# First stage of a hybrid SSD and gated-MLP layer: even rows' weights in two pieces around h, a pair's ada chunks in one burst, the pair's last chunk in two transfers, fewer warm-up matmuls

## The chip, the core and the metric

The kernel runs on one core of a Trainium2 chip. The metric is the device time of one execution in microseconds (us); the median of three runs of the kernel before is 986.98 us. The core has five engines that run side by side: TensorE (PE: matmuls; PEld is its weight load), VectorE (DVE), ScalarE (ACT), GpSimd (POOL) and SyncE (SP), which here only issues DMA transfers. All transfers run on 16 DMA engines that the queues share.

## The reference, cut to what matters

One layer works on 256 latent tokens `x` and 256 context tokens `ctx`, with 2048 features each.

```
shift, scale, gate       = split(silu(c)     @ w_ada + b_ada, 3)
shift_c, scale_c, gate_c = split(silu(c_ctx) @ w_ada + b_ada, 3)
hc = rmsnorm(ctx, g_pre) * (1 + scale_c) + shift_c
zc = hc @ w_in[:, :XBC_W + DT_W]
hx = rmsnorm(x, g_pre) * (1 + scale) + shift
zx = hx @ w_in
# then a convolution, two SSD scans, a gated MLP and the output projection
```

Everything is in float32. The kernel gets its precision by splitting each factor of a product into a rounded high part and a low part (`hi`, `lo`), and sums three products of the parts.

## The kernel before, in words

**The first stage** holds about the first 125 us. It makes the modulation (`shift` and `scale` for 16 slices of 128 features), the normalized input `h` of both token groups (512 columns), and the first seven output tiles of `w_in` with the 64 `dt` columns. It runs over 16 rows (`kt`): row k is the contraction over the features of slice k, and all its tiles add up in PSUM (`psdt` for the `dt` columns, `psx0` to `psx5` for the seven tiles, numbered 0 to 6 below; tiles 3 and 6 have 256 columns and share the bank `psx3`, the others 512). Behind it come the other tiles of `w_in`, the scans and the output projection; the change does not touch them.

**Data.** Four transfers bring the tokens (`xT`), 32 transfers of 1 MiB the columns of `w_ada` for shift and scale (`ada_0` to `ada_31`, "chunks"), 16 of 480 KB the rows' weights (`wst0` to `wst15`). SP issues them in the order of the program. Chunks lie in six buffers, rows' weights in three, and a transfer waits for its buffer.

**Modulation.** Rows 0 to 3 have two chunks each (`ada_rows`, step `r`, then `k`, `g`, `o`). From row 4 on, a pair of rows (4 and 5, 6 and 7, ...) has four. The first goes through VectorE as eight products with an accumulated sum (`ada_part`, step `v`, line 262) and a bias (`b`, line 268). The other three go through TensorE (`ada_mm`, step `a`, line 253, tile `psada`). `ada_fin` (step `f`, lines 275 and 278) transposes the result and adds the two shares into `hab`, the scale and shift of both rows of the pair.

**One row.** `scale_x` (`x`, line 388) multiplies `xT` by the norm. `make_h` (`h`, line 395: four halves on ACT) or `make_hs` (`hs`, lines 401 and 402: two halves on ACT, two on VectorE) writes `hhi` and the full value into `xT`. `make_hl` (`e`, line 405) writes `hlo`, their difference. `split_hi` (`c`, line 377) casts the row's weights, `split_dt` (`d`, line 381) and `split_lo` (`l`, line 385) write low parts. TensorE then runs `psdt` (line 455), the first three tiles (`p` and `q`, lines 475 to 478) and the tiles 3 to 6 (`m`, lines 143 to 145).

**What sets the order.** Inside the stage the engines' orders are the program's own (`manual_schedule`). `row_steps(kt)` lists the steps that are written out during row kt: the row's own matmuls and the preparation of row n = kt + 1. `m0` is `psdt` and the first three tiles, `m1` tiles 3 to 6. For an odd kt, row n is the first of a pair.

**Before the rows**, TensorE sums the squares of `xT` (line 341) and runs warm-up matmuls between them (`warm`, tile `psw`, line 319).

Of the kernel before, what the change touches and what calls it, by code (L numbers as in the profile page):

```python
# [11 lines left out]
AF = mybir.ActivationFunctionType  # L12
ALU = mybir.AluOpType
# [4 lines left out]
KT = D // P  # L18
# [29 lines left out]
def tile_hybrid_ssd_mlp(  # L48
# [30 lines left out]
    def load_raw(src, name):  # L79
        raw = wp["raw"].tile([P, 2048], F32, tag="raw", name=name)  # L80
        nc.sync.dma_start(raw, src)
        return raw
# [47 lines left out]
    hab = stp.tile([P, KT, 2, 2], F32, name="hab")  # L130
# [7 lines left out]
    hhi = [hpool.tile([P, TOK], F32R, name=f"hhi{k}") for k in range(KT)]  # L138
# [17 lines left out]
    def yseg(j):  # L156
        return y[:, j // 4, (j % 4) * 512 : (j % 4 + 1) * 512]
# [6 lines left out]
    zt, e = yseg(5)[:, 0:256], yseg(5)[:, 256:512]  # L164
# [12 lines left out]
    xT = stx.tile([P, KT, TOK], F32, name="xT")  # L177
# [15 lines left out]
    ada_raw = {}  # L193
# [62 lines left out]
    def ada_part(u, i):  # L256

        q, v = divmod(i, 2)
        if i == 0:
            part[u] = ada_raw.pop(4 * u - 2 * NSING), st2.tile([P, 4, 2], F32, tag="part", name=f"part{u}")  # L260
        raw, acc = part[u]
        nc.vector.scalar_tensor_tensor(cbj, raw[:, q * 512 : (q + 1) * 512], 1.0, cb[v], op0=ALU.mult, op1=ALU.mult,
                                       accum_out=acc[:, q, v : v + 1])
# [23 lines left out]
    def wst_load(kt):  # L287
        w = st3.tile([P, WST], F32, tag="wst", name=f"wst{kt}")
        nc.sync.dma_start(w, wst[kt])
        wraw[kt] = w  # L290

    for t in range(4):
        nc.sync.dma_start(xT[:, 4 * t : 4 * t + 4, :].rearrange("p k t -> p (k t)"), xch[t])

    ada_load(0)

    def ada_load2(c):
        ada_raw[c] = raw = wp["raw"].tile([P, 2048], F32, tag="raw", name=f"ada_{c}")
        for hf in range(2):
            nc.sync.dma_start(raw[:, hf * 1024 : (hf + 1) * 1024], wada[c][:, hf * 1024 : (hf + 1) * 1024])  # L300
# [16 lines left out]
    def warm(*ns):  # L317
        for n in ns:
            nc.tensor.matmul(psw[:, 0:n], lhsT=ones, rhs=ones[:, 0:1].to_broadcast([P, n]), start=True, stop=True)  # L319
# [53 lines left out]
    def split_hi(kt, a=0, b=WST):  # L373
        if a == 0:
            sp0[kt] = (wp["spl"].tile([P, WST + 64], F32R, tag="hi", name=f"hi_st{kt}"),
                       wp["spl"].tile([P, WST - 64], F32R, tag="lo", name=f"lo_st{kt}"))
        nc.scalar.copy(sp0[kt][0][:, 64 + a : 64 + b], wraw[kt][:, a:b])  # L377
# [5 lines left out]
    def split_lo(kt, a=64, b=WST):  # L383
        hi, lo = sp0[kt]
        nc.vector.tensor_tensor(lo[:, a - 64 : b - 64], wraw[kt][:, a:b], hi[:, 64 + a : 64 + b].bitcast(F32), op=ALU.subtract)
# [2 lines left out]
        nc.vector.scalar_tensor_tensor(xT[:, kt, :], xT[:, kt, :], pc[:, C_GPRE + kt : C_GPRE + kt + 1], rb,  # L388
                                       op0=ALU.mult, op1=ALU.mult)

    def make_h(kt):
        sl = (slice(256, 512), slice(0, 256))
        for t in (hhi[kt], xT[:, kt, :]):
            for v, s in enumerate(sl):
                nc.scalar.activation(t[:, s], xT[:, kt, s], AF.Identity, bias=hab[:, kt, 1, v : v + 1],
                                     scale=hab[:, kt, 0, v : v + 1])

    def make_hs(kt):
        a, b = hab[:, kt, 0], hab[:, kt, 1]
        for t in (hhi[kt], xT[:, kt, :]):  # L400
            nc.scalar.activation(t[:, 256:512], xT[:, kt, 256:512], AF.Identity, bias=b[:, 0:1], scale=a[:, 0:1])
# [92 lines left out]
    scale_x(2)  # L494
    for kt in range(KT):
        cs = (2 * kt + 6, 2 * kt + 7) if kt + 3 < KT else ()
        if kt < NSING - 2:
            wst_load(kt + 2)
        ada_load(*cs)
        if NSING - 2 <= kt < KT - 2:  # L500
            wst_load(kt + 2)
        for what, i in row_steps(kt):
            step(kt, what, i)
        if kt == 6:
            nc.scalar.dma_start(dtc, dtp[0:1].partition_broadcast(P))
            nc.scalar.dma_start(A, dtp[1:2].partition_broadcast(P))
            nc.scalar.dma_start(dsk, dskip.partition_broadcast(P))
# [625 lines left out]
    for blk in range(16):  # L1133
# [46 lines left out]
    op1 = ctx.enter_context(mkpool(name="op1", bufs=1))  # L1180
# [36 lines left out]
    for i in range(8):  # L1217
        tk, b = divmod(i, 4)
# [156 lines left out]
```

## Time and profile before

| What | Value |
|---|---|
| Three runs | 986.9, 986.98, 988.93 us |
| The profiled execution, its own time | 987.21 us |
| Its span | 985.5 us |
| TensorE busy | 977.1 us (99%) |
| VectorE, ACT busy | 655.8 us, 501.9 us |
| First psdt of row 0, of row 15 | 22.91 us, 122.61 us |
| DMA in 40 to 60 us | 418 GB/s, share 1.01 |

The span is that of the instructions; 1.7 us of the execution's time lie around it. Matmuls are pipelined, so a row's duration (0.39 us for 512 columns) is longer than the step from one start to the next (0.23 us), and PE counts as busy while it waits a little. Starts are therefore what to compare. In a row of the time line stand the start in us, the duration in us (for "x2" of both), engine, line, operation, what is written and read, shapes, and in brackets idle time of the engine with what ended it.

### The profile page before, as it was taken

To read this page: it belongs to the slowest core of one execution; us is meant where nothing else is said; L and a number is where in the kernel's file an instruction comes from. 1 tells how busy PE (TensorE), PEld (TensorE's weight loads), DVE (VectorE), ACT (ScalarE), POOL (GpSimd) and SP (SyncE) were. 2 spreads that over 40 slices of the span, in tenths; PEclk is the share of its full clock that TensorE was granted. 3 is DMA by queue.
4 is the path that set the end of the run, shared out by engine and by line. 5 is a ranking of instruction groups with operands and counts; after the bars stand their busy time and mean duration, and the time that the engine had idled before them with its cause. 6 is when DMAs were issued, how large, how long until landed. Compare 5 with 4: busy or idle time off the path is not lost.

```text
span 985.5 us, 13637 instructions
## 1 busy us (share of the span) xinstructions
PE 977.1 (99%) x5310; PEld 786.6 (80%) x5310; DVE 655.8 (67%) x1041; ACT 501.9 (51%) x758; POOL 112.5 (11%) x162
## 2 busy tenths in 40 slices
PE   9999999999999999999999999999999999999997
PEld 3778888778887878787888888887888888888885
DVE  5887798768886665756767766767555564445636
ACT  4344458566565454645444434555565563345522
POOL 0000002532462122124000000000000000000000
PEclk9999999999999999999999999999999999999999
DMA  9999943232323423146788777764455545556722
GB/s 372 419 418 415 388 153 134 97 144 103 128 90 134 161 85 129 44 171 217 296 304 281 283 269 270 296 259 171 170 190 195 175 167 213 188 197 231 281 86 86
DMA packets 31985, 207.26 MB, mean 210 GB/s; under 512 B 4128, under 2 KB 4384, under 8 KB 8496
## 3 DMA queue, kind: packets, MB, share of 16 engines
q1 hardware_dynamic: 28800, 192.71, 52.1%
q0 software_dynamic: 2112, 12.65, 3.7%
q10 hardware_dynamic: 1008, 1.02, 0.3%
q8 instruction: 42, 0.69, 0.3%
q14 instruction: 23, 0.19, 0.1%
HBM read 204.20 MB, written 2.16 MB: 209 GB/s over the span
## 4 chain that ended last, share of the span: by engine, by line
PE 96%; DVE 1%; ACT 1%; issue 0%; ACTq 0%
PE pa L1152 12%; PE pa L1154 12%; PE pa L1153 12%; PE psx L143 9%; PE psx L145 9%; PE psx L144 9%; PE pm L1199 3%; PE pm L1201 3%; PE pm L1200 3%; PE pq L1201 2%; PE pq L1200 2%; PE pq L1199 2%; PE psada L253 2%; PE psc L822 1%; PE pso L875 1%; PE psw L319 1%
## 5 line engine op out<-in xcount | busy, mean ns | idle before, releaser
L88 DVE TENSOR_TENSOR lo_w<-w,hi_w 128x1024 fp32r<-128x1024 f32 x173 | 210.3, 1223 | 142.1 <-ACT hi_w L87 142.0
L87 ACT CAST hi_w<-w 128x1024 fp32r<-128x1024 f32 x173 | 182.1, 1053 | 204.0 <-PE pa L1154 132.7
L1152 PE MATMUL pa<-hi_w,hhi 128*128 128x512 f32 x512 | 202.3, 395 | 0.0
L1154 PE MATMUL pa<-hi_w,hlo 128*128 128x512 f32 x512 | 199.5, 390 | 0.0
L1153 PE MATMUL pa<-lo_w,hhi 128*128 128x512 f32 x512 | 199.3, 389 | 0.0
L143 PE MATMUL psx<-hhi,hi_w 128*128 128x512 f32 (+1 forms) x400 | 153.4, 383 | 0.0
L145 PE MATMUL psx<-hhi,lo_w 128*128 128x512 f32 (+1 forms) x400 | 145.9, 365 | 0.0
L144 PE MATMUL psx<-hlo,hi_w 128*128 128x512 f32 (+1 forms) x400 | 145.7, 364 | 0.0
L1152 PEld LDWEIGHTS pa<-hi_w,hhi 128*128 128x128 f32 x512 | 96.2, 188 | 20.5 <-issue 1.6
L1154 PEld LDWEIGHTS pa<-hi_w,hlo 128*128 128x128 f32 x512 | 96.1, 188 | 20.3
L1153 PEld LDWEIGHTS pa<-lo_w,hhi 128*128 128x128 f32 x512 | 96.2, 188 | 19.4 <-issue 0.2
L620 DVE SCALAR_TENSOR_TENSOR xbc<-psx,pc,xbc 128x248 f32<-128x248 f32 (+1 forms) x204 | 83.6, 473 | 34.8 <-ACT xbc L604 33.8
L545 DVE TENSOR_TENSOR lo_w<-w,hi_w 128x1024 fp32r<-128x1024 f32 x61 | 77.1, 1271 | 23.6 <-ACT hi_w L539 23.6
L143 PEld LDWEIGHTS psx<-hhi,hi_w 128*128 128x128 f32 x400 | 75.5, 189 | 13.4 <-issue 2.9
L145 PEld LDWEIGHTS psx<-hhi,lo_w 128*128 128x128 f32 x400 | 75.4, 188 | 12.5
L144 PEld LDWEIGHTS psx<-hlo,hi_w 128*128 128x128 f32 x400 | 75.6, 189 | 12.2 <-issue 1.7
L539 ACT CAST hi_w<-w 128x1024 fp32r<-128x1024 f32 x61 | 63.5, 1044 | 26.0 <-PE psx L144 12.9
L1010 DVE SCALAR_TENSOR_TENSOR junk<-gate,cb 128x2048 bf16<-128x2048 f32 x16 | 36.7, 2292 | 26.3 <-DMA gate<-in_wada_dram 26.3
L1199 PE MATMUL pm<-hi_w,hhi 128*128 128x512 f32 x128 | 50.0, 390 | 0.0
L1200 PE MATMUL pm<-lo_w,hhi 128*128 128x512 f32 x128 | 49.9, 390 | 0.0
L1201 PE MATMUL pm<-hi_w,hlo 128*128 128x512 f32 x128 | 49.6, 389 | 0.0
L377 ACT CAST hi_st<-wst 128x960 fp32r<-128x960 f32 (+2 forms) x17 | 16.0, 942 | 45.0 <-DMA wst<-in_wst_dram 45.0
(269 smaller groups left out, 1395.7 us busy)
## 6 DMA issues: line engine op xcount, KB each, us to landing
w<-in_wlat_dram SPq DMA_DIRECT2D x64, 1024.0 KB, 4.8
w<-in_wout_dram SPq DMA_DIRECT2D x32, 1024.0 KB, 4.8
ada<-in_wada_dram SPq DMA_DIRECT2D x30, 1024.0 KB, 12.6
w<-in_wxbc_dram SPq DMA_DIRECT2D x25, 1024.0 KB, 4.8
gate<-in_wada_dram SPq DMA_DIRECT2D x16, 1024.0 KB, 5.6
R<-acs POOLq DMA_DIRECT2D x8, 1024.0 KB, 5.0
wst<-in_wst_dram SPq DMA_DIRECT2D x15, 480.0 KB, 11.9
xT<-in_xch_dram SPq DMA_DIRECT2D x4, 1024.0 KB, 7.9
```

The costliest lines, as they stand in the source:

```text
L87: nc.scalar.copy(hi, raw)
L88: nc.vector.tensor_tensor(lo, raw, hi.bitcast(F32), op=ALU.subtract)
L143: nc.tensor.matmul(ps, lhsT=whi, rhs=hhi[k][:, s], start=start, stop=False)
L144: nc.tensor.matmul(ps, lhsT=whi, rhs=hlo[k][:, s], start=False, stop=False)
L145: nc.tensor.matmul(ps, lhsT=wlo, rhs=hhi[k][:, s], start=False, stop=stop)
L620: nc.vector.scalar_tensor_tensor(ao, zi, cw[:, k : k + 1], ao, op0=ALU.mult, op1=ALU.add)
L1152: nc.tensor.matmul(pa[tk], lhsT=hhi[k][:, t], rhs=whi[:, w], start=k == 0, stop=False)
L1153: nc.tensor.matmul(pa[tk], lhsT=hhi[k][:, t], rhs=wlo[:, w], start=False, stop=False)
L1154: nc.tensor.matmul(pa[tk], lhsT=hlo[k][:, t], rhs=whi[:, w], start=False, stop=k == KT - 1)
L1199: nc.tensor.matmul(p, lhsT=yh[:, t], rhs=whi[:, w], start=j == 0, stop=False)
L1200: nc.tensor.matmul(p, lhsT=yh[:, t], rhs=wlo[:, w], start=False, stop=False)
L1201: nc.tensor.matmul(p, lhsT=yl[:, t], rhs=whi[:, w], start=False, stop=hf == 0 and j == 15)
```

## The change

- Warm-ups: after each four square sums stands one `warm`, of 256 columns after the first two groups, 512 after the last two.
- Even rows' weights (and rows 1 to 3) are cast and split in two pieces: the first 448 columns (`c1`, `l1`) ahead of or around the first half of `h`, the rest (`c2`, `l2`) behind `h`. `make_h` and `make_hs` take one half at a time (`hhi`, then `xT`).
- Rows 12 and 14 make `h` by `make_hs` in place of `make_h`; rows 8 and 10 keep `make_h`.
- A pair's three TensorE chunks run in one burst behind tiles 3 and 4, with tiles 5 and 6 behind them (for row 4's pair the burst is parted by tile 4). Before, one chunk stood ahead of the row, two behind the first three tiles, and four tiles behind those.
- In row 0, tile 4 moves ahead of the next row's chunks.
- `scale_x` of rows 12 to 15 moves to other rows (`XROW`).
- The last chunk of each pair comes in two transfers of 512 KB. An odd row's weights are loaded ahead of the second chunk of the next pair, not behind it.

```diff
-XROW = ((3, 4, 5, 6), (7, 8, 9, 10, 11), (), (12, 13), (), (14, 15))
+XROW = ((3, 4, 5, 6), (7, 8, 9, 10, 11), (12,), (), (), (), (), (13,), (), (14, 15))
...
     def ada_load(*cs):
         for ci in cs:
-            ada_raw[ci] = load_raw(wada[ci], f"ada_{ci}")
+            if ci >= 2 * NSING and ci % 4 == 3:
+                ada_load2(ci)
+            else:
+                ada_raw[ci] = load_raw(wada[ci], f"ada_{ci}")
...
         if g == 3:
-            if k != 11:
-                warm(512)
-            if k < 12:
-                warm(256)
+            warm(512 if k > 8 else 256)
...
+    def make_hs(kt, i):
         a, b = hab[:, kt, 0], hab[:, kt, 1]
-        for t in (hhi[kt], xT[:, kt, :]):
-            nc.scalar.activation(t[:, 256:512], xT[:, kt, 256:512], AF.Identity, bias=b[:, 0:1], scale=a[:, 0:1])
-            nc.vector.tensor_scalar(t[:, 0:256], xT[:, kt, 0:256], a[:, 1:2], b[:, 1:2], op0=ALU.mult, op1=ALU.add)
+        t = (hhi[kt], xT[:, kt, :])[i]
+        nc.scalar.activation(t[:, 256:512], xT[:, kt, 256:512], AF.Identity, bias=b[:, 0:1], scale=a[:, 0:1])
+        nc.vector.tensor_scalar(t[:, 0:256], xT[:, kt, 0:256], a[:, 1:2], b[:, 1:2], op0=ALU.mult, op1=ALU.add)
...
+        s_ = [("s", (n, i)) for i in range(2)]
+        c1, c2, l1, l2 = [(w, n) for w in ("c1", "c2", "l1", "l2")]
         if n < NSING:
             r = [("r", 2 * n), ("r", 2 * n + 1)]
-            q = 8 if n == 1 else 6
+            q, f = (8, m1[1:2]) if n == 1 else (6, [])
             v = [("v", (NSING, i)) for i in range(4)] if n == NSING - 1 else []
-            return (m0[:q] + r + [c_, ("k", n), d_, ("l1", n)] + m1[:1] + [("g", n), ("o", n), ("hs", n), ("l2", n)] + (v[:2] or x[:1])
-                    + [e_] + v[2:] + (x if v else x[1:]) + m0[q:] + m1[1:])
+            return (m0[:q] + f + r + [c1, ("k", n), d_, l1] + m1[:1] + [("g", n), ("o", n)] + s_ + [c2, e_, l2] + v + x
+                    + m0[q:] + m1[1 + len(f):])
...
         a = [("a", c) for c in range(p + 1, p + 4)]
-        t = v + [("f", u), h_ if n > NSING + 2 else ("hs", n), d_, l_, e_] + x + [("h", n + 1)]
+        s_ = [("h" if n in (8, 10) else "s", (n, i)) for i in range(2)]
+        t = v + [c1, ("f", u), d_, s_[0], l1, s_[1], e_, c2, l2] + x + [("h", (n + 1, i)) for i in range(2)]
         if n == NSING:
-            return m0[:5] + a[:2] + m0[5:] + m1[:1] + a[2:] + [c_] + t + m1[1:]
-        return a[:1] + m0 + a[1:] + [c_] + t + m1
+            return m0 + m1[:1] + a[:2] + m1[1:2] + a[2:] + t + m1[2:]
+        return m0 + m1[:2] + a + t + m1[2:]
...
         cs = (2 * kt + 6, 2 * kt + 7) if kt + 3 < KT else ()
-        if kt < NSING - 2:
+        q = 0 if kt < NSING - 2 else 1 if kt % 2 else 2
+        ada_load(*cs[:q])
+        if kt < KT - 2:
             wst_load(kt + 2)
-        ada_load(*cs)
-        if NSING - 2 <= kt < KT - 2:
-            wst_load(kt + 2)
+        ada_load(*cs[q:])
```

What it moves, as the instructions stand. TensorE, kernel before, from the end of row 4 into row 5 (`hhi5` belongs to row 5, `psada5` collects the chunks of the pair 6 and 7):

```order
L145 MATMUL psx3_325<-hhi4_121,lo_st4_619 128x256
L253 MATMUL psada5_697<-ada_13_551,sc_159 32x128 x16
L455 MATMUL psdt_321<-hhi5_122,hi_st5_658 128x512
L475 MATMUL psx0_322<-hhi5_122,hi_st5_658 128x512
L476 MATMUL psx0_322<-hhi5_122,lo_st5_659 128x512
```

The same place in the changed kernel:

```order
L145 MATMUL psx3_323<-hhi4_121,lo_st4_630 128x256
L457 MATMUL psdt_319<-hhi5_122,hi_st5_662 128x512
L477 MATMUL psx0_320<-hhi5_122,hi_st5_662 128x512
L478 MATMUL psx0_320<-hhi5_122,lo_st5_663 128x512
L477 MATMUL psx1_321<-hhi5_122,hi_st5_662 128x512
```

Chunk 13 no longer stands between the two rows. TensorE inside row 5, kernel before:

```order
L478 MATMUL psx2_324<-hlo5_138,hi_st5_658 128x512
L253 MATMUL psada5_697<-ada_14_651,sc_159 32x128 x16
L253 MATMUL psada5_697<-ada_15_653,sc_159 32x128 x16
L143 MATMUL psx3_325<-hhi5_122,hi_st5_658 128x256
L144 MATMUL psx3_325<-hlo5_138,hi_st5_658 128x256
L145 MATMUL psx3_325<-hhi5_122,lo_st5_659 128x256
L143 MATMUL psx4_326<-hhi5_122,hi_st5_658 128x512
```

In the changed kernel, from the end of tile 4 to row 6:

```order
L145 MATMUL psx4_324<-hhi5_122,lo_st5_663 128x512
L256 MATMUL psada5_718<-ada_13_556,sc_159 32x128 x16
L256 MATMUL psada5_718<-ada_14_654,sc_159 32x128 x16
L256 MATMUL psada5_718<-ada_15_656,sc_159 32x128 x16
L143 MATMUL psx5_325<-hhi5_122,hi_st5_662 128x512
L144 MATMUL psx5_325<-hlo5_138,hi_st5_662 128x512
L145 MATMUL psx5_325<-hhi5_122,lo_st5_663 128x512
L143 MATMUL psx3_323<-hhi5_122,hi_st5_662 128x256
L144 MATMUL psx3_323<-hlo5_138,hi_st5_662 128x256
L145 MATMUL psx3_323<-hhi5_122,lo_st5_663 128x256
L457 MATMUL psdt_319<-hhi6_123,hi_st6_772 128x512
```

The three chunks now follow each other, and two tiles stand between them and row 6 where four stood. VectorE, kernel before, from the preparation of row 3 to that of row 4 (`part4` is the share of chunk 8, `adat4` its pair's transposed sum):

```order
L402 TENSOR_SCALAR xT_156<-xT_156,hab_110 128x256
L385 TENSOR_TENSOR lo_st3_514<-wst3_413,hi_st3_513 128x512
L262 SCALAR_TENSOR_TENSOR y_68,part4_532<-ada_8_415,y_68 128x512 x2
L405 TENSOR_TENSOR hlo3_136<-xT_156,hhi3_120 128x512
L262 SCALAR_TENSOR_TENSOR y_68,part4_532<-ada_8_415,y_68 128x512 x6
L268 TENSOR_TENSOR part4_532<-part4_532,bab_111 128x8
L275 STREAM_TRANSPOSE adat4_626<-psada4_563 128x128
```

The changed kernel:

```order
L401 TENSOR_SCALAR xT_156<-xT_156,hab_110 128x256
L404 TENSOR_TENSOR hlo3_136<-xT_156,hhi3_120 128x512
L385 TENSOR_TENSOR lo_st3_515<-wst3_412,hi_st3_514 128x512
L265 SCALAR_TENSOR_TENSOR y_68,part4_535<-ada_8_414,y_68 128x512 x4
L388 SCALAR_TENSOR_TENSOR xT_156<-xT_156,pc_87,y_68 128x512
L265 SCALAR_TENSOR_TENSOR y_68,part4_535<-ada_8_414,y_68 128x512 x4
L271 TENSOR_TENSOR part4_535<-part4_535,bab_111 128x8
L278 STREAM_TRANSPOSE adat4_632<-psada4_572 128x128
```

`hlo3` and the second piece of `lo_st3` now stand ahead of all eight products, and a `scale_x` between them.

ACT, kernel before, the preparation of rows 8 and 9:

```order
L377 CAST hi_st8_902<-wst8_797 128x960
L395 ACTIVATE hhi8_125<-xT_156,hab_110 128x256 x2
L395 ACTIVATE xT_156<-xT_156,hab_110 128x256 x2
L395 ACTIVATE hhi9_126<-xT_156,hab_110 128x256 x2
L395 ACTIVATE xT_156<-xT_156,hab_110 128x256 x2
L377 CAST hi_st9_943<-wst9_840 128x960
```

The changed kernel:

```order
L377 CAST hi_st8_918<-wst8_802 128x448
L394 ACTIVATE hhi8_125<-xT_156,hab_110 128x256 x2
L394 ACTIVATE xT_156<-xT_156,hab_110 128x256 x2
L377 CAST hi_st8_918<-wst8_802 128x512
L394 ACTIVATE hhi9_126<-xT_156,hab_110 128x256 x2
L394 ACTIVATE xT_156<-xT_156,hab_110 128x256 x2
L377 CAST hi_st9_952<-wst9_843 128x960
```

Half of row 8's cast has moved behind row 8's `h` and ahead of row 9's.

More of the change, by code (lines that the diff above doesn't have):

```diff
@@ L389, in scale_x, with make_h @@
                                        op0=ALU.mult, op1=ALU.mult)
-    def make_h(kt):
-        sl = (slice(256, 512), slice(0, 256))
-        for t in (hhi[kt], xT[:, kt, :]):
[L394 to L398, printed above, removed]
+    def make_h(kt, i):
+        t = (hhi[kt], xT[:, kt, :])[i]
+        for v, s in enumerate((slice(256, 512), slice(0, 256))):
+            nc.scalar.activation(t[:, s], xT[:, kt, s], AF.Identity, bias=hab[:, kt, 1, v : v + 1],
+                                 scale=hab[:, kt, 0, v : v + 1])
+    def make_hs(kt, i):
         a, b = hab[:, kt, 0], hab[:, kt, 1]
-        for t in (hhi[kt], xT[:, kt, :]):
-            nc.scalar.activation(t[:, 256:512], xT[:, kt, 256:512], AF.Identity, bias=b[:, 0:1], scale=a[:, 0:1])
-            nc.vector.tensor_scalar(t[:, 0:256], xT[:, kt, 0:256], a[:, 1:2], b[:, 1:2], op0=ALU.mult, op1=ALU.add)
+        t = (hhi[kt], xT[:, kt, :])[i]
+        nc.scalar.activation(t[:, 256:512], xT[:, kt, 256:512], AF.Identity, bias=b[:, 0:1], scale=a[:, 0:1])
+        nc.vector.tensor_scalar(t[:, 0:256], xT[:, kt, 0:256], a[:, 1:2], b[:, 1:2], op0=ALU.mult, op1=ALU.add)
     def make_hl(kt):
@@ L444, in row_steps @@
         a = [("a", c) for c in range(p + 1, p + 4)]
-        t = v + [("f", u), h_ if n > NSING + 2 else ("hs", n), d_, l_, e_] + x + [("h", n + 1)]
+        s_ = [("h" if n in (8, 10) else "s", (n, i)) for i in range(2)]
+        t = v + [c1, ("f", u), d_, s_[0], l1, s_[1], e_, c2, l2] + x + [("h", (n + 1, i)) for i in range(2)]
         if n == NSING:
-            return m0[:5] + a[:2] + m0[5:] + m1[:1] + a[2:] + [c_] + t + m1[1:]
-        return a[:1] + m0 + a[1:] + [c_] + t + m1
-    STEPS = {"a": ada_mm, "f": ada_fin, "v": lambda ui: ada_part(*ui), "b": ada_bias, "r": ada_rows, "x": scale_x, "e": make_hl, "hs": make_hs, "k": ada_keep, "g": ada_sum, "o": ada_one,
-             "h": make_h, "c": split_hi, "d": split_dt, "l": split_lo,
+            return m0 + m1[:1] + a[:2] + m1[1:2] + a[2:] + t + m1[2:]
+        return m0 + m1[:2] + a + t + m1[2:]
+    STEPS = {"a": ada_mm, "f": ada_fin, "v": lambda ui: ada_part(*ui), "b": ada_bias, "r": ada_rows, "x": scale_x, "e": make_hl, "s": lambda ni: make_hs(*ni), "k": ada_keep, "g": ada_sum, "o": ada_one,
+             "h": lambda ni: make_h(*ni), "c": split_hi, "c1": lambda n: split_hi(n, 0, WH), "c2": lambda n: split_hi(n, WH), "d": split_dt, "l": split_lo,
              "l1": lambda n: split_lo(n, 64, WH), "l2": lambda n: split_lo(n, WH)}
@@ L487, in tile_hybrid_ssd_mlp @@
     ada_fin(0)
-    make_hs(0)
+    make_hs(0, 0)
     split_lo(0, 64, WH)
+    make_hs(0, 1)
     make_hl(0)
```

## The prediction

> **What bounds the kernel now.** I read the page first.
>
> ```profile
> PE 977.1 (99%) x5310; PEld 786.6 (80%) x5310; DVE 655.8 (67%) x1041; ACT 501.9 (51%) x758; POOL 112.5 (11%) x162
> ...
> PE 96%; DVE 1%; ACT 1%; issue 0%; ACTq 0%
> ```
>
> TensorE holds 96% of the chain that ended last, so a microsecond by which it leaves the first stage earlier or later should reach the end undiminished. The change touches the first stage alone. The table of stretches shows what limits that stage (columns: time, PE, PEld, DVE, ACT, POOL busy, clock, DMA share, GB/s):
>
> ```profile
> 40.00:60.00 20.00, 19.74 (x227) 14.82 (x225) 18.10 (x44) 7.78 (x13) 0.00 (x0) 1.00 1.01 418
> ...
> 80.00:100.00 20.00, 20.00 (x204) 16.08 (x205) 14.86 (x36) 9.62 (x17) 0.00 (x0) 1.00 1.02 417
> ```
>
> TensorE and the 16 DMA engines are both full. Then TensorE in order of time. Each row k of the stage starts with `psdt<-hhi`; the rows below are the starts of rows 3, 4, 6, 8, 9, 10, 12, 14 and 15, with the ada pieces inside row 9.
>
> ```profile
> 45.60 0.40 PE L455 MATMUL psdt<-hhi,hi_st 128*128 128x512 f32 x1
> ...
> 53.84 0.46 PE L455 MATMUL psdt<-hhi,hi_st 128*128 128x512 f32 x1
> ...
> 66.94 0.40 PE L455 MATMUL psdt<-hhi,hi_st 128*128 128x512 f32 x1
> ...
> 79.90 0.50 PE L455 MATMUL psdt<-hhi,hi_st 128*128 128x512 f32 x1
> ...
> 85.81 0.50 PE L455 MATMUL psdt<-hhi,hi_st 128*128 128x512 f32 x1
> ...
> 88.57 1.96 PE L253 MATMUL psada<-ada,sc 128*32 128x128 f32 x64
> 90.45 0.39 PE L143 MATMUL psx<-hhi,hi_st 128*128 128x256 f32 x1
> ...
> 92.63 0.40 PE L455 MATMUL psdt<-hhi,hi_st 128*128 128x512 f32 x1
> ...
> 105.27 0.40 PE L455 MATMUL psdt<-hhi,hi_st 128*128 128x512 f32 x1
> ...
> 117.86 0.39 PE L455 MATMUL psdt<-hhi,hi_st 128*128 128x512 f32 x1
> ...
> 122.61 0.40 PE L455 MATMUL psdt<-hhi,hi_st 128*128 128x512 f32 x1
> ```
>
> A pair of rows took 13.1 (4 to 6), 13.0, 12.7, 12.6 and 12.6 us. Its parts: a bare row 122.61 - 117.86 = 4.75; the first three tiles 88.57 - 85.81 = 2.76; the other four tiles 92.63 - 90.45 = 2.18, half of it two tiles; two ada chunks 1.88, so three 2.82. Sum 12.5, against 12.6 measured: matmuls stand back to back. No large stall is there to remove, only 0.1 us at each switch to or from ada work and the late rows 4 to 8. What counts is whether the new order opens stalls.
>
> **Part 1: fewer warm-ups, row 0 in a new order.** Before:
>
> ```profile
> 15.91 0.70 PE L319 MATMUL psw<-ones 128*128 128x256 f32 x2
> ...
> 19.63 0.57 ACT L377 CAST hi_st<-wst 128x448 fp32r<-128x448 f32 x1 [0.25 <-DMA wst<-in_wst_dram]
> ...
> 19.04 0.33 SPq L81 DMA_DIRECT2D ada<-in_wada_dram  x1
> ...
> ada<-in_wada_dram SPq DMA_DIRECT2D x1, 1024.0 KB, 14.0
> ...
> 33.01 1.93 PE L224 MATMUL psada<-ada,sc 128*32 128x256 f32 x32
> 34.87 0.39 PE L143 MATMUL psx<-hhi,hi_st 128*128 128x256 f32 x1
> ```
>
> A 256-column warm-up takes 0.6 to 0.7. Two 512s go and one 256 becomes a 512, so the square sums end about 1.3 to 1.4 sooner. Row 0 gains that: its weights landed at 19.6 and are cast by 20.2, which leaves it room. But data takes part of it back. Chunk 5 lands at 19.04 + 14.0 = 33.0, and its half of the 1.93 burst cannot end before 33.05 + 0.97 = 34.0, against 34.87. So rows 2 and 3 come 0.85 sooner: row 3 at 44.75.
>
> **Part 2: row 4.** The path from the last ada matmul to the next row, seen here with row 4's own rows, and the hand-over to TensorE seen at row 0:
>
> ```profile
> 50.98 1.08 PE L253 MATMUL psada<-ada,sc 128*32 128x128 f32 x32
> 52.00 0.50 PE L143 MATMUL psx<-hhi,hi_st 128*128 128x512 f32 x1
> ...
> 52.13 0.32 DVE L275 STREAM_TRANSPOSE adat<-psada 128x128 f32<-128x128 f32 x1 [0.27 <-PE psada L253]
> 52.49 0.17 DVE L278 TENSOR_TENSOR hab<-adat,part 128x8 f32<-128x8 f32 x1
> 52.69 0.60 ACT L401 ACTIVATE hhi<-xT,hab 128x256 fp32r<-128x256 f32 x1
> 53.33 0.60 ACT L401 ACTIVATE xT<-xT,hab 128x256 f32<-128x256 f32 x1
> ...
> 22.26 0.60 ACT L401 ACTIVATE hhi<-xT,hab 128x256 fp32r<-128x256 f32 x1 [2.06 <-DVE hab L278]
> ...
> 22.91 0.50 PE L455 MATMUL psdt<-hhi,hi_st 128*128 128x512 f32 x1
> ```
>
> Call A the time at which TensorE goes on after ada work (52.00). The transpose follows at A + 0.13, `hhi` is ready at 53.29, and TensorE takes it 0.05 later: A + 1.35 at the soonest. Before, four or three tiles (2.18, 1.84) stood behind the ada work and covered this. Now two do, 1.05 + 0.1 for the switch = 1.15. Every pair's even row now waits 0.2.
>
> At row 4 VectorE decides:
>
> ```profile
> 44.60 0.60 ACT L401 ACTIVATE xT<-xT,hab 128x256 f32<-128x256 f32 x1
> 45.35 0.69 DVE L262 SCALAR_TENSOR_TENSOR y<-ada,y 128x512 f32<-128x512 f32 x1
> 51.70 0.17 DVE L268 TENSOR_TENSOR part<-part,bab 128x8 f32<-128x8 f32 x1
> ...
> 53.60 1.08 DVE L385 TENSOR_TENSOR lo_st<-wst,hi_st 128x896 fp32r<-128x896 f32 x1
> ...
> 55.21 1.41 DVE L388 SCALAR_TENSOR_TENSOR xT<-xT,pc,y 128x512 f32<-128x512 f32 x2
> ```
>
> From 45.35 to 51.70 it ran eight partial products and one `hlo`; (6.35 - 0.6) / 8 is 0.73 for each. Now `hlo` of row 3 and the second half of `lo` come first. `hlo` needs ACT's `xT`, done at 45.20 - 0.85 = 44.35; two steps of 0.6 put the products at 45.55. Eight of them (5.9) and the `scale_x(12)` that now stands between (0.7) end at 52.1, so the transpose goes at 52.25, not at the 51.55 that TensorE would allow (its burst ends near 51.4). Row 4: 52.25 - 0.13 + 1.35 = 53.47, a gain of 0.35 in place of 0.85.
>
> **Part 3: row 5.** Before, chunk 13's matmuls stood ahead of row 5; now row 5 follows row 4 at once, at 53.47 + 4.75 = 58.2. Count from A = 52.1. ACT: `hhi` at A + 0.7, `xT` at 1.35, the second cast at 1.85, row 5's four halves from 2.35 to 4.4, its cast to 5.3. VectorE: `hlo` of row 5 at A + 4.45, then the two products that `row_steps` still puts ahead of `d` (1.5), then `d` ends at A + 6.75 = 58.9 and `lo`, one piece of 1.08, at 59.9. `psdt` waits 0.7, the first low product waits to 59.95, another 0.4. Nine of the eleven matmuls at 0.23, two tiles (1.05), the switch and three chunks (2.9) end at A = 66.0, row 6 at 67.4: 0.45 LATER than before.
>
> **Part 4: the later pairs.** With the short form (`s`: rows 6, 12, 14): 1.35 + 4.7 + 0.1 (row n+1's low piece) + 2.6 + 1.05 + 2.8 = 12.6, what they took before: the saved switches pay for the new wait. Rows 8 and 10 keep `h`, all on ACT:
>
> ```profile
> 103.97 1.10 ACT L395 ACTIVATE hhi<-xT,hab 128x256 fp32r<-128x256 f32 x2 [1.82 <-DVE hab L278]
> ...
> 107.93 0.98 ACT L377 CAST hi_st<-wst 128x960 fp32r<-128x960 f32 x1
> ```
>
> Two halves take 1.10, not 0.60, so the row starts at A + 1.85. ACT then has eight halves of 0.5, the new second cast (0.5) and the odd row's cast: done at A + 6.15; VectorE's `d` and `lo` to A + 7.4, while TensorE wants `lo` at A + 7.0: 0.45 more. A pair is 1.85 + 4.7 + 0.45 + 2.6 + 1.05 + 2.8 = 13.45, of which 0.85 is loss. Row 12 again starts by the short path.
>
> A: 66.0, 78.6, 92.05, 105.5, 118.1. Rows 8, 10, 12, 14 at 80.45, 93.9, 106.85, 119.45; against before +0.55, +1.3, +1.6, +1.6; row 15 and all behind it +1.6.
>
> Costed at nothing: the cast in two pieces (0.57 + 0.6 for 0.98 on ACT, 0.55 + 0.68 for 1.08 on VectorE) beyond its place above, since ACT is idle half the time; `scale_x` 13, 14 and 15, which fit the 1.3 us that VectorE waits for row n+1's `xT`; six more issues on SP at 0.33, which mostly waits; the burst's late release of chunks, since transfers in flight then still fill 5 us. A split chunk is bounded by:
>
> ```profile
> 13.00:15.00 2.00, 2.00 (x16) 0.76 (x12) 1.29 (x2) 1.15 (x2) 0.00 (x0) 1.00 1.04 442
> 15.50:18.00 2.50, 2.50 (x19) 0.87 (x12) 0.79 (x2) 0.00 (x0) 0.00 (x0) 1.00 1.02 360
> ...
> 102.34 0.33 SPq L81 DMA_DIRECT2D ada<-in_wada_dram  x1
> ...
> ada<-in_wada_dram SPq DMA_DIRECT2D x1, 1024.0 KB, 9.9
> ```
>
> The lower row holds mostly half chunks. 1 MiB at 360 instead of 418 GB/s costs 0.4, at least nothing; six make chunk 31 land at 112.2 + 2.4 = 114.6 at worst. Its matmuls start near 117: hidden, zero taken. "DMA: Bandwidth & Descriptors" of the Trainium skill ("Anatomy of one DMA", a fit for the gpsimd path) gives about 2.0 us fixed for each transfer, and its rules ask for at least 1 MiB; laid end to end, six splits would add 12 us and the time would be near 995. The 360 GB/s row disagrees: half a chunk in 1.46 us holds no 2 us of its own.
>
> **Sum.** The profiled execution took 987.21 (span 985.5), 0.23 above the median 986.98. +1.6 gives 988.8, and 988.6 beside the median. About 0.2%, 2 us, is what a measurement of this kernel can tell from no change; the forecast lies just inside.
>
> **Rivals.**
> - *Faster: the joint is covered.* If `hhi` of the even row is there before the two tiles behind the burst are done, TensorE runs through: row 3 at 44.75, row 4 at 52.6, five pairs of 12.4, row 14 at 114.6: -3.3, 983.7 beside the median. For it: the burst does save a switch, and chunk 31's 112.2 allows it. Against it: the path of 1.35 against 1.15. It decides where that path is 0.2 shorter (0.7 at rows 8 and 10) and VectorE is ready at row 4.
> - *No change.* The front's gain goes at row 4 and 5 as computed, but the `h` rows cost what they did: row 14 near +0.4 to -0.4, 987.0. ACT's queue of eight halves speaks against it.
> - *Slower: the clock falls between the thinned warm-ups.* One row at half rate would add up to 4.7, less what the data waits absorb: +3 over the forecast, 991.6. The rows say 1.00 throughout, but show no stretch this thin.
> - *Slower: splits cost a fixed time each.* Above 0.9 us each, chunk 31 passes the 117 at which it is wanted; at 2 us the end is 6.6 later, near 995.
>
> **How the numbers follow.** Forecast 0.54, its own range 987.4 to 989.8 (faster than +2 us 0.31, slower 0.23); covered joint 0.24 (0.18 beyond -2 us, 0.06 within); no change 0.12; clock 0.05; splits 0.05. So faster 0.18, same 0.49, slower 0.33. The range 985.0 to 990.4 leaves out half of the covered case and the last two.
>
> **What would show it.** Right: row 3 near 44.8, row 4 near 53.5 with the transpose behind the products, row 5's `psdt` and first low product waiting about 1.1 together, rows 8 and 10 waiting 0.7 on ACT's `hhi`, rows 9 and 11 on `lo`, row 14 near 119.5. Wrong: rows 4 to 14 that start without a wait on `hhi`, a half clock before 20 us, or TensorE waiting for ada data behind 60 us.

## The result, and the profile after

The changed kernel takes 989.51 us (median of 19 runs, 988.61 to 990.52), the kernel before 987.08 (19 runs beside them). The ratio is 1.0021, with a 95% interval of 1.0014 to 1.0028: slower by 2.4 us. That is clear of no change by the interval, and just past the 2 us that the prediction took as the least that can be told. The profiled execution took 989.25, its span 987.5. On its page TensorE is busy 0.5 less than the 977.1 before, with four instructions fewer; those are the two warm-ups that went:

```profile
PE 976.6 (99%) x5306; PEld 786.3 (80%) x5306; DVE 657.3 (67%) x1051; ACT 500.3 (51%) x763; POOL 112.5 (11%) x162
```

The stretches that the prediction quoted (time, PE, PEld, DVE, ACT, POOL busy, clock, DMA share, GB/s) now read:

```profile
40.00:60.00 20.00, 18.83 (x189) 14.44 (x178) 17.42 (x45) 7.84 (x15) 0.00 (x0) 1.00 1.02 415
80.00:100.00 20.00, 19.18 (x171) 15.01 (x172) 16.07 (x37) 10.23 (x19) 0.00 (x0) 1.00 1.02 413
```

TensorE is busy 0.9 and 0.8 us less of 20 than before; the transfers ran as before. Where it idles, its time line tells (starts of rows 3, 4, 5, 6, 8, 10, 12, 14 and 15, a burst, and two first low products):

```profile
44.41 0.40 PE L457 MATMUL psdt<-hhi,hi_st 128*128 128x512 f32 x1
...
52.94 0.50 PE L457 MATMUL psdt<-hhi,hi_st 128*128 128x512 f32 x1 [0.46 <-ACT hhi L400]
...
58.28 0.50 PE L457 MATMUL psdt<-hhi,hi_st 128*128 128x512 f32 x1 [0.44 <-DVE hi_st L381]
...
59.28 0.50 PE L478 MATMUL psx<-hhi,lo_st 128*128 128x512 f32 x1 [0.27 <-DVE lo_st L385]
...
62.60 2.83 PE L256 MATMUL psada<-ada,sc 128*32 128x128 f32 x96
65.36 0.50 PE L143 MATMUL psx<-hhi,hi_st 128*128 128x512 f32 x1
...
66.70 0.50 PE L457 MATMUL psdt<-hhi,hi_st 128*128 128x512 f32 x1
...
78.06 0.50 PE L143 MATMUL psx<-hhi,hi_st 128*128 128x512 f32 x1
...
79.89 0.50 PE L457 MATMUL psdt<-hhi,hi_st 128*128 128x512 f32 x1 [0.51 <-ACT hhi L394]
...
93.43 0.50 PE L457 MATMUL psdt<-hhi,hi_st 128*128 128x512 f32 x1 [0.51 <-ACT hhi L394]
...
99.05 0.50 PE L478 MATMUL psx<-hhi,lo_st 128*128 128x512 f32 x1 [0.17 <-DVE lo_st L385]
...
106.47 0.51 PE L457 MATMUL psdt<-hhi,hi_st 128*128 128x512 f32 x1
...
119.17 0.50 PE L457 MATMUL psdt<-hhi,hi_st 128*128 128x512 f32 x1
123.91 0.40 PE L457 MATMUL psdt<-hhi,hi_st 128*128 128x512 f32 x1
```

Each wait has the name that the prediction gave it: rows 4, 8 and 10 wait for ACT's `hhi`, row 5 for the low part of its `dt` columns and then for `lo`, row 11 for `lo` (and row 9, without a mark: its first low product starts at 85.52, 0.3 late, and `lo` is done at 85.47). From where TensorE goes on after the burst to the next row it is 66.70 - 65.36 = 1.34 with the short form and 79.89 - 78.06 = 1.83 with `h`. VectorE at rows 4 and 5:

```profile
45.25 0.69 DVE L265 SCALAR_TENSOR_TENSOR y<-ada,y 128x512 f32<-128x512 f32 x1
...
48.06 0.75 DVE L388 SCALAR_TENSOR_TENSOR xT<-xT,pc,y 128x512 f32<-128x512 f32 x1
...
51.66 0.17 DVE L271 TENSOR_TENSOR part<-part,bab 128x8 f32<-128x8 f32 x1
51.74 0.31 DVE L278 STREAM_TRANSPOSE adat<-psada 128x128 f32<-128x128 f32 x1
...
56.05 0.69 DVE L404 TENSOR_TENSOR hlo<-xT,hhi 128x512 fp32r<-128x512 f32 x1 [1.14 <-ACT xT L394]
...
58.01 0.22 DVE L381 TENSOR_TENSOR hi_st<-wst,hi_st 128x64 fp32r<-128x64 f32 x1
58.14 1.08 DVE L385 TENSOR_TENSOR lo_st<-wst,hi_st 128x896 fp32r<-128x896 f32 x1
```

The transpose follows the last product at once, as forecast, though TensorE's chunks were done at 51.17.

| Start of | before | predicted | after | the same again |
|---|---|---|---|---|
| row 0 | 22.91 | 21.5 to 21.6 | 21.70 | 21.55 |
| row 3 | 45.60 | 44.75 | 44.41 | 44.54 |
| row 4 | 53.84 | 53.47 | 52.94 | 53.05 |
| row 6 | 66.94 | 67.4 | 66.70 | 66.80 |
| row 8 | 79.90 | 80.45 | 79.89 | 79.99 |
| row 10 | 92.63 | 93.9 | 93.43 | 93.54 |
| row 12 | 105.27 | 106.85 | 106.47 | 106.59 |
| row 14 | 117.86 | 119.45 | 119.17 | 119.28 |

### The profile page after: what moved, and what is told of

It reads as the page before. It is cut to its first block, busy times and chain, and to the rows that moved or that the text cites. A ratio compares the mean times of both kernels' runs of the same rounds, so it can differ in the third digit from the quotient of the medians.

```text
span 987.5 us, 13652 instructions
## 1 busy us (share of the span) xinstructions
PE 976.6 (99%) x5306; PEld 786.3 (80%) x5306; DVE 657.3 (67%) x1051; ACT 500.3 (51%) x763; POOL 112.5 (11%) x162
## 4 chain that ended last, share of the span: by engine, by line
PE 73%; issue 10%; DMA 6%; DVE 6%; ACT 3%; POOL 1%; DVEq 0%; POOLq 0%; ACTq 0%
PE psx L143 9%; PE psx L145 8%; PE psx L144 8%; PE pa L1155 5%; PE pa L1157 5%; PE pa L1156 5%; DMA gate<-in_wada_dram 5%; PE pm L1202 3%; PE pm L1203 3%; PE pm L1204 3%; DVE lo_w L88 2%; PE pq L1202 2%; PE pq L1203 2%; PE pq L1204 2%; PE psada L256 2%
## 5 line engine op out<-in xcount | busy, mean ns | idle before, releaser
L145 PEld LDWEIGHTS psx<-hhi,lo_w 128*128 128x128 f32 x400 | 75.4, 189 | 12.6
L377 ACT CAST hi_st<-wst 128x448 fp32r<-128x448 f32 (+2 forms) x26 | 17.6, 676 | 43.6 <-DMA wst<-in_wst_dram 31.0
```

What stands on the lines that cost most here:

```text
L145: nc.tensor.matmul(ps, lhsT=wlo, rhs=hhi[k][:, s], start=False, stop=stop)
```

## The experiments

The runs came in three groups of four, each beside its own runs of the kernel before: medians 987.17 (33 runs), 987.18 (28) and 987.02 (33). My theory was that of the prediction: the even row's joint with two tiles, ACT's `h` at rows 8 and 10, row 5's products, each costing what was worked out. The rivals: preparation in pieces, split transfers, data or VectorE as the real limit.

**The changed kernel again (x7_again).**

> The changed kernel once more, as it is, beside the others on the same chip. Theory (a part of the 2.4 is chance of the executions: rows 0 to 3 move by 0.4 with the landing of chunk 5, the transposes at 647 by up to 1.5): span median 986.9 to 987.2, time 988.9 to 989.5, row 6 between 66.6 and 67.1, row 14 between 119.0 and 119.7. Rival (all of it is the program's): 989.5 and rows within 0.1 of the first profile.

989.28 (988.66 to 990.96), ratio 1.0023 (1.0013 to 1.0033), median span 987.0. Every row lies within 0.15 of the first profile. Row 15 is 1.39 later than before and the end of TensorE's work 1.38; in the first profile another 0.7 was lost behind 560 us, half of it at the transposes near 647, and that did not come again. So all of the loss inside the span is the first stage's; the late part was chance.

**The chunks back in their places (x2_noburst).**

```diff
-            return m0 + m1[:1] + a[:2] + m1[1:2] + a[2:] + t + m1[2:]
-        return m0 + m1[:2] + a + t + m1[2:]
+            return m0[:5] + a[:2] + m0[5:] + m1[:1] + a[2:] + t + m1[1:]
+        return a[:1] + m0 + a[1:] + t + m1
```

> The changed kernel with the three chunks of a pair back in their old places (one ahead of the odd row, two behind its first three tiles, four tiles behind them); all else stays. Theory (the loss is the joint, covered by two tiles where the path needs 1.35 or 1.85): no even row waits on hhi, pairs take 12.65 in place of 13.2, 13.5, 13.05 and 12.7, chunk 13 ahead of row 5 covers that row's waits; row 4 stays near 52.95, row 6 near 65.6, row 14 near 116.1 (3.1 sooner than the changed kernel, 1.8 sooner than the kernel before): 986.4. Rival (the loss is in the preparation: ACT's eight halves, the casts in two pieces, VectorE's order): pairs stay above 13 and the end within 0.7 of 989.5.

986.09, ratio to before 0.9988 (0.9979 to 0.9997): 3.3 below the changed kernel by the two ratios. Row 6 at 65.87, row 14 at 116.66. The pairs took 12.54 (6 to 8), 12.95, 12.76 and 12.54, so the theory holds but for the two middle ones. There a second limit shows. VectorE, and TensorE's row 10, in this run:

```profile
76.37 0.32 DVE L278 STREAM_TRANSPOSE adat<-psada 128x128 f32<-128x128 f32 x1
...
79.19 0.69 DVE L404 TENSOR_TENSOR hlo<-xT,hhi 128x512 fp32r<-128x512 f32 x1 [1.29 <-ACT xT L394]
...
81.69 0.69 DVE L404 TENSOR_TENSOR hlo<-xT,hhi 128x512 fp32r<-128x512 f32 x1 [0.54 <-ACT xT L394]
...
89.58 0.17 DVE L271 TENSOR_TENSOR part<-part,bab 128x8 f32<-128x8 f32 x1
89.66 0.31 DVE L278 STREAM_TRANSPOSE adat<-psada 128x128 f32<-128x128 f32 x1
```

```profile
91.35 0.50 PE L457 MATMUL psdt<-hhi,hi_st 128*128 128x512 f32 x1 [0.22 <-ACT hhi L394]
```

VectorE waits twice for ACT's eight halves, 1.29 and 0.54, and gets from one transpose to the next only in 13.29; the chunks were done at 88.80 and the transpose waited for the products.

**One tile more behind the burst (x5_three).**

```diff
-            return m0 + m1[:1] + a[:2] + m1[1:2] + a[2:] + t + m1[2:]
-        return m0 + m1[:2] + a + t + m1[2:]
+            return m0 + a[:2] + m1[:1] + a[2:] + t + m1[1:]
+        return m0 + m1[:1] + a + t + m1[1:]
```

> The changed kernel with the burst one tile sooner, so that three tiles (1.95 with the switch) stand between it and the even row; all else stays. Theory (cover first, and behind it VectorE in the pairs whose even row is made by ACT alone): rows 6 and 14 start on time (pairs 6 to 8 and 12 to 14 near 12.6), but in the two pairs from row 8 and row 10 VectorE needs 13.35 from one transpose to the end of its next eight products, as the run with the chunks in their old places shows, so those pairs keep 13.2 to 13.4: row 14 near 117.6, end 987.7 to 988.0. Rival (cover is all that was missing): every pair 12.5, row 14 near 116.5, end 986.8. Second rival (the burst's place does not matter): 989.5.

986.95, ratio 0.9997 (0.9989 to 1.0006). Row 14 at 117.31; the pairs 12.27, 13.15, 12.88, 12.28. The two pairs with `h` are VectorE's:

```profile
77.31 0.31 DVE L278 STREAM_TRANSPOSE adat<-psada 128x128 f32<-128x128 f32 x1
...
90.37 0.17 DVE L271 TENSOR_TENSOR part<-part,bab 128x8 f32<-128x8 f32 x1
90.46 0.31 DVE L278 STREAM_TRANSPOSE adat<-psada 128x128 f32<-128x128 f32 x1
```

13.15 again, with the products right ahead of the transpose. The theory's order of limits is borne out by the rows; its time was 0.8 to 1.0 too long, and by the time alone the first rival (986.8) was nearer.

**The short form at rows 8 and 10 (x3_s).**

```diff
-        s_ = [("h" if n in (8, 10) else "s", (n, i)) for i in range(2)]
+        s_ = [("s", (n, i)) for i in range(2)]
```

> The changed kernel with the short form of h also at rows 8 and 10. Theory: the waits of rows 8 and 10 on ACT's hhi (0.5 each) and of rows 9 and 11 on lo (0.3 each) go, pairs 6 to 8, 8 to 10 and 10 to 12 take 12.7 each, row 14 comes 1.6 to 1.8 sooner: 987.8. Rival (VectorE, which takes two of the four halves over, becomes the late one): row 8 and 10 start 0.3 sooner at most, end 989.0 or later.

987.48, ratio 1.0003 (0.9994 to 1.0012). TensorE's rows 8, 10, 12 and 14:

```profile
79.56 0.50 PE L457 MATMUL psdt<-hhi,hi_st 128*128 128x512 f32 x1
...
92.29 0.50 PE L457 MATMUL psdt<-hhi,hi_st 128*128 128x512 f32 x1
...
104.99 0.50 PE L457 MATMUL psdt<-hhi,hi_st 128*128 128x512 f32 x1
...
117.67 0.50 PE L457 MATMUL psdt<-hhi,hi_st 128*128 128x512 f32 x1
```

All pairs take 12.7 (the changed kernel: 13.19, 13.54, 13.04, 12.70), 1.7 less in sum. The prediction had put 2 x 0.85 on these rows.

**Row 5's low parts first (x4_row5).**

```diff
-            if n == NSING + 1:
-                return [e_, c_] + v[:2] + [d_, l_] + v[2:] + m0 + m1
             return [e_, c_, d_, l_] + v + m0 + m1
```

> The changed kernel with row 5's low parts ahead of its two partial products. Theory: row 5 starts near 57.7 without its wait on the low part of the dt columns (0.45), and its first low product does not wait either (0.27); row 6 comes 0.7 to 0.9 sooner and the end too: 988.7. Rival (the products, now later, hold up the transpose of the next pair, or chunk 15's landing takes it back): row 6 within 0.2 of 66.7, end 989.5.

987.97, ratio 1.0009 (1.0001 to 1.0018). Rows 4, 5 and 6:

```profile
53.33 0.50 PE L455 MATMUL psdt<-hhi,hi_st 128*128 128x512 f32 x1 [0.44 <-ACT hhi L400]
58.07 0.40 PE L455 MATMUL psdt<-hhi,hi_st 128*128 128x512 f32 x1
66.03 0.50 PE L455 MATMUL psdt<-hhi,hi_st 128*128 128x512 f32 x1
```

From row 4 to row 6 it is 12.70 in place of 13.75: both waits of row 5, 1.05 together (the prediction: 1.1). Row 3 came 0.4 later than in the first profile, so row 6 moved 0.67 only. The time moved more than that: it is 1.3 below the changed kernel's in x7_again and 0.7 below what was expected. Of the 1.3, 0.7 lies in the span (median 986.3 against 987.0), the rest around it.

**The fewer warm-ups: alone (x1_warm), and undone (x9_oldwarm).** The first is the kernel before with

```diff
-            if k != 11:
-                warm(512)
-            if k < 12:
-                warm(256)
+            warm(512 if k > 8 else 256)
```

and the second the changed kernel with the same lines the other way round.

> The kernel before with the fewer warm-ups alone. Theory (the thinner front is a gain by itself, and chunks cap it): rows 0 to 2 start about 1.2 sooner (row 0 near 21.7); at row 3 chunk 10, which lands near 47.5, and chunk 11, near 50.0, hold TensorE, so row 4 comes 0.5 to 0.8 sooner and the end too: 986.3 to 986.6 against 987.1. Rival A (all of it reaches the end): row 4 at 52.6, end 985.9. Rival B (row 4 takes all of it back): row 4 at 53.8, end 987.1.

> The changed kernel with the old warm-ups. Theory (at rows 1 to 3 the fewer warm-ups and the new preparation each give a part; the warm-ups alone gave 0.16 behind row 2): row 0 near 22.8, row 1 near 30.3, row 3 near 45.3, which is 0.8 later than with fewer warm-ups, and as much at the end: row 14 near 120.0, 990.0. Rival (chunks hold the front, so warm-ups make no difference there): row 3 at 44.5, row 14 at 119.3, 989.3.

Alone: 986.94, ratio 0.9998 (0.9989 to 1.0007). My theory of a gain of half a microsecond fell: row 0 came 1.64 sooner, row 1 0.61, and from row 2 on only 0.16. (Of the 1.64, 0.54 is chance: the square sums began at 8.41, not at 8.95, see the last section.) Its TensorE shows where the rest went:

```profile
26.59 0.64 PE L224 MATMUL psada<-ada,sc 128*32 128x256 f32 x8 [0.64 <-DMA ada<-in_wada_dram]
...
32.18 0.50 PE L452 MATMUL psdt<-hlo,hi_st 128*128 128x512 f32 x1 [0.33 <-DVE hlo L402]
...
32.85 1.93 PE L224 MATMUL psada<-ada,sc 128*32 128x256 f32 x32
```

It waits for chunk 3, which lands at 26.54, then for row 1's `hlo`, so that row 1's burst begins only when chunk 5 has landed as well (32.82). In the changed kernel tile 4 stands in the wait for chunk 3, row 1's `hlo` stands ahead of its second low piece and of a `scale_x`, and the burst begins 1.2 sooner, with chunk 4:

```profile
31.06 0.40 PE L457 MATMUL psdt<-hlo,hi_st 128*128 128x512 f32 x1
...
31.62 2.13 PE L227 MATMUL psada<-ada,sc 128*32 128x256 f32 x32
```

so that it ends 1.05 behind chunk 5, not 1.9. The gain at rows 2 and 3 comes with the new order: row 3 starts at 44.41 to 44.82 in all eleven profiles with the new order, at 45.36 to 45.60 in the three with the old.

Undone: 989.17, ratio 1.0023 (1.0014 to 1.0032). Row 0 at 21.66, row 3 at 44.45, row 14 at 119.21, as the rival said, but for a reason that neither had. The third of TensorE's first warm-ups, two instructions, in this run and in the kernel before:

```profile
4.61 1.03 PE L322 MATMUL psw<-ones 128*128 128x512 f32 x2
```

```profile
4.70 1.92 PE L319 MATMUL psw<-ones 128*128 128x512 f32 x2
```

The same two instructions take 1.03 and 1.92: TensorE came to full pace sooner here. The square sums began at 7.70, not at 8.95, and row 0 stood 13.96 behind that, as in both other profiles with the old warm-ups. So this trace cannot price the warm-ups at row 3. The median span is 987.4 against 987.0 and 987.1 with fewer; that hints at 0.3 to 0.4, but the groups ran on different chips.

**The loads: without the split (x6_nosplit), and alone in the kernel before (x10_loads).**

```diff
-            if ci >= 2 * NSING and ci % 4 == 3:
-                ada_load2(ci)
-            else:
-                ada_raw[ci] = load_raw(wada[ci], f"ada_{ci}")
+            ada_raw[ci] = load_raw(wada[ci], f"ada_{ci}")
```

is the first. The second has the changed kernel's `ada_load` and load order, and the rest of the kernel before.

> The changed kernel with each pair's last chunk in one transfer of 1 MiB again. Theory (halves cost the stream nothing, and nothing waits for the second half): rows as in the changed kernel, row 14 within 0.4 of 119.2, and the span's median within 0.3 of 987.1. Rival A (each split costs the queue time): the stream ends 1 to 2 sooner than 115.0, without a gain for TensorE. Rival B (the six added transfers lengthen what lies around the span, which reaches 1.9 to 2.8 in half of the changed kernel's runs and 1.7 in all of the kernel before): it is back at 1.65 to 1.8 in all runs, and the median 0.4 to 0.6 below that of the changed kernel beside it.

> The kernel before with the loads of the changed one alone: each pair's last chunk in two transfers, an odd row's weights ahead of the next pair's second chunk. Theory (the stream of chunks has slack in that kernel): rows within 0.3 of those before, row 14 at 117.6 to 118.0, 987.0 to 987.3, and 1.65 to 1.8 around the span in all runs. Rival (the loads are what makes the time around the span uneven): 1.9 to 2.8 in a third of the runs or more, median 987.4 or above.

988.86 (ratio 1.0022, 1.0012 to 1.0032) and 987.17 (1.0005, 0.9996 to 1.0014). The first is 0.4 below the changed kernel beside it, as rival B said, but the median spans are alike (987.1 and 987.0) and 3 of its 8 runs still have more than 1.85 around the span, so the rival's reason does not hold. Without the split row 14 is at 119.33, against 119.28 in the repeated profile; with the loads alone it is at 117.37, 0.49 sooner than before (its row 0 was 0.57 sooner by chance), and the median does not move. A split chunk's halves land 1.28 apart (85.13, 86.41, 87.70 for chunk 22 and the halves of 23 in the first profile), a whole one takes 2.5: over the six split chunks a split costs 0.05 to 0.14. The Trainium skill, "DMA: Bandwidth & Descriptors" ("Anatomy of one DMA"), gives about 2.0 us fixed for each transfer on the gpsimd path. In this queue, which SP fills and which is always full, the runs show none of it.

**A version with the parts that held (x8_three_fixes, x11_x15, x12_two).** The edits to the changed kernel are x5_three's and x3_s's, and

```diff
-XROW = ((3, 4, 5, 6), (7, 8, 9, 10, 11), (12,), (), (), (), (), (13,), (), (14, 15))
+XROW = ((3, 4, 5, 6), (7, 8, 9, 10, 11), (), (12,), (), (), (), (13,), (), (14, 15))
...
-            if n == NSING + 1:
-                return [e_, c_] + v[:2] + [d_, l_] + v[2:] + m0 + m1
-            return [e_, c_, d_, l_] + v + m0 + m1
+            return v[:1] + [e_, c_, d_, l_] + v[1:] + m0 + m1
```

In x11_x15 the last entry is `(14,), (), (15,)`; x12_two is x11_x15 with the burst where the changed kernel has it.

> The changed kernel with four edits: three tiles behind the burst, the short form of h at all even rows, row 5's products behind its low parts and one product of every pair in the gap ahead of the odd row's hlo, scale_x of row 12 moved from row 2 to row 3. Theory (cover plus VectorE's chain): row 4 near 52.4, row 6 near 65.2, every pair 12.5, row 14 near 115.2, end 984.5 to 984.9, below both kernels. Rival A (data): chunk 31, which landed at 112.6, is wanted at 112.8, so the stream holds the last pairs and row 14 is 116 or later: 985.5. Rival B (VectorE still late): rows 8 to 14 lose 0.2 each, 985.6.

> The version with three tiles behind the burst and the fixes, with scale_x of row 15 moved from row 9 to row 11 (beside that of row 14 it delayed row 11's low part by 0.3). Theory: row 11 no longer waits on lo, the pair 10 to 12 takes 12.5 to 12.6 in place of 13.0, row 14 near 115.1, where chunk 31 (112.5) allows no less: 985.4 to 985.6. Rival (the chunks set these pairs, not VectorE): row 14 within 0.15 of 115.5, 985.9.

> The same version with the burst where the changed kernel has it, two tiles ahead of the even row. Theory (path 1.35 against a cover of 1.15): every even row waits 0.2 to 0.3 on hhi, pairs take 12.65 to 12.75, row 14 near 116.1: 986.2 to 986.5. Rival (chunks set the pairs; the later burst gives them room and costs nothing): row 14 within 0.2 of that with three tiles, 985.5.

x8_three_fixes: 985.89, ratio 0.9985 (0.9976 to 0.9993); row 4 at 52.59, row 14 at 115.48, 0.3 later than forecast, and the time 1.0 to 1.4 above the forecast (its median span is 983.7). Row 11 waited 0.3 on `lo` behind two `scale_x`. x11_x15 took that away: 985.22, ratio 0.9980 (0.9971 to 0.9989), faster than both kernels. x12_two: 986.10, 0.9991 (0.9982 to 1.0000). Rows 4, 6, 12 and 14, of x11_x15 and then of x12_two:

```profile
52.70 0.47 PE L455 MATMUL psdt<-hhi,hi_st 128*128 128x512 f32 x1
...
65.20 0.47 PE L455 MATMUL psdt<-hhi,hi_st 128*128 128x512 f32 x1
...
102.91 0.47 PE L455 MATMUL psdt<-hhi,hi_st 128*128 128x512 f32 x1
...
115.32 0.47 PE L455 MATMUL psdt<-hhi,hi_st 128*128 128x512 f32 x1
```

```profile
52.71 0.50 PE L455 MATMUL psdt<-hhi,hi_st 128*128 128x512 f32 x1
...
65.39 0.50 PE L455 MATMUL psdt<-hhi,hi_st 128*128 128x512 f32 x1
...
103.49 0.50 PE L455 MATMUL psdt<-hhi,hi_st 128*128 128x512 f32 x1
...
116.16 0.50 PE L455 MATMUL psdt<-hhi,hi_st 128*128 128x512 f32 x1
```

The two start row 4 together and differ by 0.84 at row 14: the price of the joint with two tiles, 0.17 for each of five even rows in the mean. It was put at 0.2. But the rows do not share it evenly (0.19 at row 6, nothing at row 8, 0.11 to 0.28 at the others), since in x11_x15 data has become the limit. Its burst in row 7, and that of x12_two:

```profile
72.89 3.08 PE L256 MATMUL psada<-ada,sc 128*32 128x128 f32 x96
75.91 0.50 PE L143 MATMUL psx<-hhi,hi_st 128*128 128x512 f32 x1
```

```profile
73.99 2.83 PE L256 MATMUL psada<-ada,sc 128*32 128x128 f32 x96
```

The burst of x11_x15 is 0.25 longer, because the second half of chunk 19 lands only at 75.29; in row 9 the same costs 0.16 (chunk 23, 87.93). TensorE goes on 0.62 behind both, and 0.64 behind the last halves of the next two pairs, where no wait shows and 0.02 is left. So without the waits for data the joint would be worth about 1.25, an estimate from these bursts. Whether still more cover gains anything was not run.

## Why the prediction was right, and where not

The time came 0.9 above the forecast, inside its range and on the side it named, and every wait that it named stands where it said. It had thought a change within 2 us likelier (0.49) than one beyond (0.33); 2.4 is beyond, and only by what lies outside the stage, as the sum below shows. By its own steps:

- **Part 1.** The cap was right, the source of the gain misnamed. Row 1's burst ends 1.05 behind chunk 5; that chunk lands at 32.5 to 32.9 in the new order, not at 33.0, and row 3 gains 0.8 to 1.2 where 0.85 was put. But the warm-ups alone give 0.16 there; the rest comes only with the new order of row 1's preparation. The prediction did not ask when row 1's `hlo` is ready. Whether the new order would give the rest without any lead at row 0 is not shown, since row 0 of x9_oldwarm was early by chance.
- **Part 2.** VectorE decides row 4, as said, 0.5 sooner than said: row 3 was 0.3 sooner and the nine steps took 6.4, not 6.55. `scale_x` of row 12 is 0.4 of it: moved on, the transpose comes at 51.31 (x8_three_fixes).
- **Part 3.** Row 5's two waits: 1.1 forecast, 1.05 measured by taking them away.
- **Part 4.** The paths were 1.35 and 1.85, measured 1.34 and 1.83. But each pair took 0.1 more than its sum (12.70 for 12.6, 13.54 for 13.45): the switch into the burst, 0.09, stood in part 3's sum and was left out here. It cost 0.4 over four pairs, and hid behind the early rows 4 to 6. In the pairs with `h` it is luck that nothing else shows: the odd row's wait on `lo` was 0.3, not 0.45, and the even row itself took 4.86, not 4.7, with a wait of 0.11 on `hlo` that was not forecast.
- **The sum.** Row 14 was put 1.6 late; it is 1.3 to 1.4 late beside the one profile of before, whose rows were themselves 0.2 to 0.5 later than with the loads or the warm-ups alone. The medians of the spans differ by 1.5 to 1.8 (987.0 and 987.1 against 985.3 to 985.5). So the stage was sized well. The term that was missing is what lies around the span: the sum takes the stage's 1.6 straight to the time, as if 1.7 lay around the span whatever the kernel. It does lie there in all 94 executions of the kernel before beside these experiments (1.66 to 1.84). In the changed kernel 16 of 28 have more than 1.85, up to 2.8, a mean of 2.1: the other 0.4.
- **The rivals.** A covered joint is what x11_x15 makes, with row 4 at 52.7 and pairs of 12.4 to 12.7: 1.8 us below before, where 3.3 was put. Splits cost TensorE nothing in the changed kernel. The clock did not fall once the square sums ran: every one lasts 0.59 to 0.62, with both sets of warm-ups.

The loss of the changed kernel, measured against x11_x15 at row 14, is 3.9: about 0.8 joint, 1.7 the `h` rows, 1.05 row 5, 0.4 `scale_x` of row 12. Each price was taken with other parts around it, so that they add up so closely is partly luck. The first is the burst's place; the others are steps around it that lost their cover, and x2_noburst, with four tiles and a chunk between the rows again, hides most of them.

## What to carry to other kernels

Before work is drawn together in one burst, write down the path from its last matmul to the next consumer, engine by engine, beside what stands behind the burst: here 1.35 or 1.85 against 1.15, and one tile more takes the 2 us back (x5_three). Cover that looks idle may hide several waits at once; when it goes, each must be found and moved (a product ahead of a low part, four halves on one engine). And a lead at the front is worth only what the next landing leaves of it: price it at the row behind the last transfer that is waited for.

## What was not expected of the hardware

**TensorE's pace at the start.** The first warm-ups start 0.85 apart, later ones 0.43, and the step down comes between 4 and 7 us, differently in each execution: over the 14 profiles the square sums begin at 7.53 to 8.95. The table of stretches reads 1.00 there, but that is no reading: the trace's records of the granted clock begin only at the step, at 4.0 to 7.0 us in the 14 profiles, and the table counts time without a record as 1.00. With the old warm-ups row 0 follows 13.96 behind, so it moves by 1.25 by chance; with fewer it stands at 21.21 to 21.75 in all eleven. The Trainium skill, "TensorE: Matmul & The Clock Gate" ("Part 1: The HAM clock gate"), says that the array runs at half rate until a window of about 3.4 us, which runs freely, has seen it busy, so that the step moves from run to run. The halved pace agrees. The step itself moves over 3 us here, more than the 0.5 us to either side that the page gives.

**The time around the span.** It is even (1.66 to 1.84) with the old warm-ups in the changed kernel (11 runs), with the fewer in the kernel before (11) and with the loads alone (11), and uneven without the splits (3 of 8 runs above 1.85). So neither the warm-ups nor the loads alone do it. What does is open. One thing goes with it: in the profiles of the four even kernels the last load of a 16 KB block of instructions comes 10.8 to 11.7 us ahead of the end; in nine of the other ten it comes within 4.3 us of the end or behind it, or does not show. That was seen, not tested, and it does not hold execution by execution: of those nine profiled executions six themselves have only 1.66 to 1.75 around the span.
